# Root mean squares of the norms: summed on every partition by one matmul, and the power taken on 256 columns

## The chip, the cores and the metric

The kernel runs on one core of one Trainium2 chip. The metric is the device time of one execution in microseconds. In the traces PE is TensorE, PEld its weight loads, DVE is VectorE, ACT is ScalarE, POOL is GpSimd, SP is SyncE.

## What is computed

Two transformer blocks in fp32, one after the other, on 256 tokens of width 1024. The first has two layers with modulated norms, attention or retention, and a gated FFN, for the tokens x and, in its first layer, a context of 256 tokens (C in the kernel). The second has two layers of FFN, a mixing stage of three branches, and FFN. What the change touches is the norm:

```python
def rms_norm(x, g):
    xf = x.astype(jnp.float32)
    y = xf * lax.rsqrt(jnp.mean(xf * xf, axis=-1, keepdims=True) + EPS)
    return (y * g.astype(jnp.float32)).astype(x.dtype)

h_x = modulate(rms_norm(x, norm1_g[i]), mx[0], mx[1])     # first block
# retention, per head of width 512:
mu = jnp.mean(o, axis=-1, keepdims=True)
var = jnp.mean(jnp.square(o - mu), axis=-1, keepdims=True)
y = ((o - mu) * lax.rsqrt(var + EPS)) ...
# second block:
x = x + 0.5 * swiglu_2(rmsnorm(x, ffn1_norm[l]), ...)
h = rmsnorm(x, mix_norm[l])
```

## The kernel before

Activations stand with features on the partitions: a tensor of 256 tokens is 128 partitions x 8 feature tiles (`KC`) x 256 columns. So a norm needs, for each column (token), a sum over partitions and feature tiles, and its result on all partitions. The squares of the feature tiles are added up by VectorE into one tile of 128x256 (`acc`, L1782); what is left is the sum over partitions.

Weights stream through SyncE's DMA queue as raw 128x2048 fp32 tiles (3 buffers), and each block of 128x1024 is split into a high part by ScalarE (L346) and a low part by VectorE (L347), 4 buffers of each. A product is then three matmuls (L351 to L353: high times high, high times low, low times high) or, in the second block, two (L359, L360, the second on half the columns). Their results go to 4 PSUM banks (`pp`); small results go to 4 others (`pa`). A scheduler sets each engine's order of instructions by its own model of the times; an engine takes its instructions strictly in that order.

A norm takes these steps. `rstd_rs` (L381): two matmuls per part with `acc` as weights and two columns of ones put the sums of 128 tokens each on 128 partitions, as 128x2 (L389); VectorE scales and adds epsilon (L392); GpSimd raises to the power -0.5 (L394, `mhalf` holds -0.5). `rstd_ps` (L397): two matmuls with the result as broadcast weights and the identity bring it back onto the columns of all partitions (L401), in PSUM. `rstd_bc` (L405) copies that to SBUF on ScalarE (L407). fp32 matmuls of 128x2 and 128x128 leave two records each in the trace.

Who uses it: `norm_mod` (five norms of the first block; it reads the PSUM bank itself in `modulated`, L519: `mu` = x times gain, L528 `mt` = `mu` times the norm, L529 high part on ScalarE, L530 low part on VectorE); the four retention heads (`outputs`, first product L1396, queued among the matmuls that make the next head's keys, whose rotary products are L1307 and L1308); the four FFNs of the second block (`ffn`, L1178, on sums that were projected without the norm); the two mixing stages (L1521). All of them are generators: a `yield` marks where another stage's matmuls are put in between.

Of the kernel before, what the change touches and what calls it, by code (L numbers as in the profile page):

```python
# [8 lines left out]
F32 = mybir.dt.float32  # L9
# [3 lines left out]
ALU = mybir.AluOpType  # L13
# [3 lines left out]
D = 1024  # L17
KC = 8
T = 256
NF = 22  # L20
EPS = 1e-6
# [61 lines left out]
def _groups(n, gs):  # L83
    out, m = [], 0
    for g in gs:
        out.append(list(range(m, m + g)))
        m += g
    assert m == n, (m, n)
    return out
# [24 lines left out]
G_FFN = _groups(NF, FFN_GROUPS + [1] * (NF - sum(FFN_GROUPS)))  # L114
# [217 lines left out]
class _Kernel:  # L332
# [74 lines left out]
        self.nc.scalar.copy(bc, self.rstd_ps(rs))  # L407
        return bc

    def rstd_steps(self, acc, inv_n, out):  # L410

        rs = self.rstd_rs(acc, inv_n)
        yield
        out.append(self.rstd_bc(rs))
        yield

    def sumsq(self, src, pool):
# [7 lines left out]
    def run(self):  # L425
        tc, nc, A = self.tc, self.nc, self.A
        with ExitStack() as es:
            P = lambda name, bufs, **kw: es.enter_context(tc.tile_pool(name=name, bufs=bufs, **kw))
            self.p_pp = P("pp", 4, space=PSUM)
            self.p_pa = P("pa", 4, space=PSUM)  # L430
            self.p_dram = P("dram", 1, space=bass.MemoryType.DRAM)
            self.p_raw = P("raw", 3)
            self.p_hl = P("hl", 4)
            self.p_base = P("base", 1)
            self.p_sm = P("sm", 2)
            base = self.p_base

            self.vec = base.tile([128, VEC.n], F32, name="vec")
            self.load(self.vec, A["vec"])
            self.ident = base.tile([128, 128], F32, name="ident")  # L440
            self.ones = base.tile([128, 128], F32, name="ones")
            nc.vector.memset(self.ones, 1.0)
            self.mhalf = base.tile([128, 2], F32, name="mhalf")
            nc.vector.memset(self.mhalf, -0.5)
            self.eps = base.tile([128, 1], F32, name="eps")
            nc.vector.memset(self.eps, EPS)
            self.identb = base.tile([128, 128], BF16, name="identb")
            self.X = base.tile([128, KC, T], F32, name="X")
            self.hh = base.tile([128, KC, 512], F32R, name="hh")
            self.hl = base.tile([128, KC, 512], F32R, name="hl_")  # L450
            self.kvd = self.p_dram.tile([128, 4097], F32, name="kvd")

            with ExitStack() as e1:
                self.p_b1 = e1.enter_context(tc.tile_pool(name="b1", bufs=1))
                self.block1()
            if self.stop is None or self.stop.startswith("b2"):
                self.block2()
# [92 lines left out]
    def norm_mod(self, l, which, s, acc):  # L550


        rs = self.rstd_rs(acc, 1.0 / D)
        yield
        bc = self.rstd_ps(rs)
        G, sh = self.gain(l, s, 1 + 3 * which, f"{l}{s}{which}"), self.ada_p(l, s, 3 * which)
        src, o = (self.X, self.C)[s], slice(256 * s, 256 * s + 256)
        for k in range(KC):
            hi, lo = self.hps(k) if l == 1 and which == 1 else (self.hh[:, k, o], self.hl[:, k, o])
            self.modulated(k, hi, lo, src[:, k], bc, G[:, k:k + 1], sh[:, k:k + 1])  # L560
        yield
# [593 lines left out]
    def ffn(self, pool, ws, acc, scal, next_g):  # L1155


        nc = self.nc
        th = pool.tile([128, NF, 512], F32R, name="th", tag="th")
        norm, bc = None, []  # L1160
        if acc is not None:
            norm = self.rstd_steps(acc, 1.0 / D, bc)
        for grp in G_FFN:
            banks = [[self.pp() for _ in range(2)] for _ in grp]
            for k in range(KC):
                x = self.hp(k)
                for i in range(len(grp)):
                    for u in range(2):
                        self.mmp(banks[i][u], ws.next(), x, k == 0, k == KC - 1)
                if norm is not None and grp is G_FFN[0] and k in (2, 4):  # L1170
                    next(norm)
            for i, m in enumerate(grp):
                src = pool.tile([128, 512], F32, name="fn", tag="fn", bufs=2)
                for u in range(2):
                    self.halves(src[:, 256 * u:256 * u + 256], banks[i][u])
                if norm is not None:
                    v = src.rearrange("p (a q) -> p a q", a=2)
                    nc.vector.tensor_mul(v, v, bc[0].unsqueeze(1).to_broadcast([128, 2, 256]))  # L1178
                s = pool.tile([128, 256], F32, name="fs", tag="fs", bufs=2)
                nc.scalar.activation(s, src[:, 0:256], AF.Silu)  # L1180
                h = pool.tile([128, 256], F32, name="fh", tag="fh", bufs=2)
                nc.vector.tensor_mul(h, s, src[:, 256:512])
                self.split(th[:, m, 0:256], th[:, m, 256:512], h)
        out_g = self.v("final") if next_g is None and self.stop is None else None
        self.acc_x = _Acc(self, self.p_sm, "accx", KC, next_g is None)
        self.proj_p(ws, G_DOWN, NF, lambda k: th[:, k], self.resid_p(scal, next_g, out_g))
# [69 lines left out]
    def retention(self, pool, norm_c, mem, ec, ez):  # L1256
        nc, A = self.nc, self.A
# [8 lines left out]
        ws = self.stream("ret")  # L1266
        tmp = lambda w: pool.tile([128, w], F32, name="tmp", tag=f"tmp{w}", bufs=3 if w == 512 else 2)

        hd = [{} for _ in range(4)]

        def decay(h):
            Dm = hd[h]["D"] = pool.tile([128, 4, 256], F32, name="Dm", tag="Dm", bufs=1)
# [91 lines left out]
        def outputs(h):  # L1364

            Ph, Pl = hd[h]["P"]
            O = pool.tile([128, 4, 256], F32, name="O", tag="O")
            acc = tmp(256)
            for mp in range(2):
                ps = self.pa()  # L1370
                vh, vl = hd[h]["v"][mp]
                for j in range(2):
                    for kt in range(4):
                        ds = slice(128 * j, 128 * j + 128)
                        self.mm3(ps[:, 256 * j:256 * j + 256], (vh[:, kt, ds], vl[:, kt, ds]), (Ph[:, kt], Pl[:, kt]),
                                 kt == 0 and j == 0, kt == 3 and j == 1)
                nc.scalar.copy(O[:, 2 * mp:2 * mp + 2].rearrange("p a q -> p (a q)"), ps)
            nc.vector.tensor_add(acc, O[:, 0], O[:, 1])
            nc.vector.tensor_add(acc, acc, O[:, 2])
            nc.vector.tensor_add(acc, acc, O[:, 3])  # L1380
            yield
            mu = self.pa()
            nc.tensor.matmul(mu[:, 0:256], lhsT=self.ones, rhs=acc, start=True, stop=True)
            ac2 = _Acc(self, self.p_sm, "accg", 4)
            for m in range(4):
                nc.vector.scalar_tensor_tensor(out=O[:, m], in0=mu[:, 0:256], scalar=-1.0 / 512, in1=O[:, m],
                                               op0=ALU.mult, op1=ALU.add)
                ac2.add(O[:, m])
            yield
            rs = self.rstd_rs(ac2, 1.0 / 512)  # L1390
            yield
            bc = self.rstd_bc(rs)
            for m in range(4):
                i = 4 * h + m
                o = O[:, m]
                nc.vector.scalar_tensor_tensor(out=o, in0=o, scalar=self.v("gn", i), in1=bc, op0=ALU.mult, op1=ALU.mult)  # L1396
                nc.vector.tensor_mul(o, o, hd[h]["g"][:, m])
                self.split(zh[:, i], zl[:, i], o)
            yield
# [35 lines left out]
        norm = self.norm_mod(1, 1, 0, self.acc_x)  # L1435
# [38 lines left out]
    def mix(self, pool, l, acc):  # L1474
        nc, A = self.nc, self.A
        tmp = lambda w, nm, bufs=1: pool.tile([128, w], F32, name=nm, tag=nm, bufs=bufs)
        com, es = pool, ExitStack()
        pool = es.enter_context(self.pool(f"mixe{l}"))
# [24 lines left out]
        ws = self.stream(f"mix_{l}")  # L1503
# [8 lines left out]
        lru = (self.hl[:, :, 0:256], self.hl[:, :, 256:512])  # L1512

        bcs = []
        norm = self.rstd_steps(acc, 1.0 / D, bcs)

        def scaled(dsts):

            def ev(grp, ps, banks):
                for i, m in enumerate(grp):  # L1520
                    nc.vector.tensor_mul(dsts[m], ps[i], bcs[0])  # L1521
            return ev

        d = {4: kf, 9: vT}
# [114 lines left out]
                next(g)  # L1639
            running[:] = [g for g in running if next(g, self) is not self] + list(new)  # L1640

        self.proj(ws, [[0, 1]], KC, self.hps, 256, scaled(d), lambda gi, k: next(norm) if k in (3, 6) else None)
        advance(mem_job(0))
        self.proj(ws, [[2, 3]], KC, self.hps, 256, scaled(d))
        advance(mem_job(1))
# [96 lines left out]
        pool = es.enter_context(self.pool(f"mixl{l}"))  # L1742
# [43 lines left out]
class _Stream:  # L1786
# [33 lines left out]
    def next(self, n=1):  # L1820
        b, j = divmod(self.i, 8)
        assert j + n <= 8
        if b == self.b:
            self.split()
        self.i += n
        s = slice(128 * j, 128 * j + 128 * n)
        return self.hi[:, s], self.lo[:, s]
# [20 lines left out]
```

## Time and profile before

| | |
|---|---|
| time, median of 3 runs | 2456.08 us (2454.55 to 2456.79) |
| time of the profiled execution | 2456.09 us |
| its span | 2454.3 us |
| TensorE busy | 2419.2 us, 99% |
| VectorE busy | 1649.7 us, 67% |
| ScalarE busy | 1252.5 us, 51% |
| GpSimd busy | 70.2 us, 3%, 90 instructions |

The span is the traced part; the time holds 1.8 us more around it. The granted TensorE clock is at its upper level all through, so times of different stages can be compared directly. Matmuls overlap at their ends, so what one costs is read from the distance of starts, not from its own duration.

### The profile page before, as it was taken

What the parts mean: (1) busy time and instruction counts of PE and PEld (TensorE: products, weight loads), DVE (VectorE), ACT (ScalarE), POOL (GpSimd) and SP (SyncE); (2) the same over time, 40 slices, a digit from 0 to 9 for tenths busy, and PEclk for the clock granted to TensorE, in tenths of its full rate; (3) what the DMA queues carried; (4) which work ended last, traced back from release to release, by engine and by line L of the source; (5) the groups of instructions that cost most, each with busy time, mean ns of one, the idle gap of its engine ahead of it and who ended that gap; (6) DMA issues with size and microseconds to landing.
All of it is one profiled execution on the core that took longest, in us unless ns stands there. A gap on an engine that the chain in (4) does not pass through costs nothing.

```text
span 2454.3 us, 38056 instructions
## 1 busy us (share of the span) xinstructions
PE 2419.2 (99%) x15304; PEld 2108.0 (86%) x15304; DVE 1649.7 (67%) x2800; ACT 1252.5 (51%) x2173; POOL 70.2 (3%) x90
## 2 busy tenths in 40 slices
PE   7999999999999999999999999999999999999998
PEld 6666698777899999988888889998888888999887
DVE  7447477653366556676687678778768766877874
ACT  4546352222254444655555467455546546845653
POOL 2310000000000000000000100000000010000000
PEclk9999999999999999999999999999999999999999
DMA  8530445653232224555555534555555553355553
GB/s 303 217 121 1 148 146 199 230 220 105 102 113 86 104 104 154 194 188 186 181 188 189 201 109 156 184 189 185 192 178 185 190 209 110 129 198 189 182 193 106
DMA packets 57825, 402.72 MB, mean 164 GB/s; under 512 B 6464, under 2 KB 7616, under 8 KB 9904
## 3 DMA queue, kind: packets, MB, share of 16 engines
q1 hardware_dynamic: 55808, 393.54, 45.2%
q0 software_dynamic: 1408, 4.65, 0.6%
q8 instruction: 120, 1.97, 0.3%
q10 hardware_dynamic: 432, 2.10, 0.2%
q14 instruction: 57, 0.47, 0.1%
HBM read 397.12 MB, written 3.15 MB: 163 GB/s over the span
## 4 chain that ended last, share of the span: by engine, by line
PE 94%; DVE 3%; ACT 2%; issue 0%; DMA 0%; POOL 0%; SPq 0%; DVEq 0%; ACTq 0%
PE pp L359 26%; PE pp L360 13%; PE pp L351 13%; PE pp L353 13%; PE pp L352 13%; PE pp L1329 1%; PE pp L1331 1%; PE pp L1330 1%; PE pp L474 1%; PE pa L968 1%; PE pp L1003 1%; PE pa L967 1%; PE pp L1022 1%; ACT whi L346 1%; PE pa L352 0%; PE pa L351 0%
## 5 line engine op out<-in xcount | busy, mean ns | idle before, releaser
L347 DVE TENSOR_TENSOR wlo<-raw,whi 128x1024 fp32r<-128x1024 f32 (+1 forms) x645 | 787.7, 1223 | 392.0 <-ACT whi L346 384.3
L346 ACT CAST whi<-raw 128x1024 fp32r<-128x1024 f32 (+1 forms) x645 | 674.9, 1049 | 697.4 <-PE pp L352 336.5
L359 PE MATMUL pp<-hh,whi 128*128 128x512 f32 x1760 | 618.2, 394 | 0.0
L351 PE MATMUL pp<-hh,whi 128*128 128x256 f32 (+1 forms) x1608 | 515.3, 321 | 3.5 <-ACT whi L346 3.5
L353 PE MATMUL pp<-hh,wlo 128*128 128x256 f32 (+1 forms) x1608 | 513.1, 320 | 2.7 <-DVE wlo L347 2.7
L360 PE MATMUL pp<-hh,wlo 128*128 128x256 f32 x1760 | 490.8, 279 | 0.0
L359 PEld LDWEIGHTS pp<-hh,whi 128*128 128x128 f32 x1760 | 329.8, 187 | 79.4 <-DVE fn L1191 1.0
L351 PEld LDWEIGHTS pp<-hh,whi 128*128 128x128 f32 x1608 | 303.5, 189 | 42.5 <-issue 16.5
L360 PEld LDWEIGHTS pp<-hh,wlo 128*128 128x128 f32 x1760 | 329.9, 187 | 0.1
L353 PEld LDWEIGHTS pp<-hh,wlo 128*128 128x128 f32 x1608 | 303.4, 189 | 25.8 <-DVE wlo L347 3.5
L352 PE MATMUL pp<-hl__87,whi 128*128 128x512 f32 (+1 forms) x936 | 321.9, 344 | 0.0
L359 PE MATMUL pp<-th,whi 128*128 128x512 f32 x880 | 309.2, 393 | 0.0
L360 PE MATMUL pp<-th,wlo 128*128 128x256 f32 x880 | 248.9, 283 | 0.0
L352 PE MATMUL pp<-hh,whi 128*128 128x256 f32 x800 | 227.9, 285 | 0.0
L359 PEld LDWEIGHTS pp<-th,whi 128*128 128x128 f32 x880 | 165.3, 188 | 38.2
L352 PEld LDWEIGHTS pp<-hl__87,whi 128*128 128x128 f32 x936 | 176.1, 188 | 23.1 <-DVE hl__87 L530 0.2
L360 PEld LDWEIGHTS pp<-th,wlo 128*128 128x128 f32 x880 | 165.4, 188 | 0.0
L352 PEld LDWEIGHTS pp<-hh,whi 128*128 128x128 f32 x800 | 151.5, 189 | 0.7 <-issue 0.3
L1190 ACT COPY fn<-pp 128x256 f32<-128x256 f32 x220 | 82.0, 374 | 125.4 <-PE pp L360 125.4
L1191 DVE TENSOR_TENSOR fn<-pp,fn 128x256 f32<-128x256 f32 x220 | 92.0, 422 | 34.5 <-ACT fn L1190 34.5
L499 DVE SCALAR_TENSOR_TENSOR ada_acc<-raw,cact,ada_acc 128x1024 f32<-128x1024 f32 x56 | 70.4, 1281 | 28.0 <-DMA raw<-in_ada 27.4
L351 PE MATMUL pp<-th,whi 128*128 128x512 f32 (+1 forms) x198 | 73.5, 371 | 0.0
(394 smaller groups left out, 3540.9 us busy)
## 6 DMA issues: line engine op xcount, KB each, us to landing
raw<-in_b2ffn SPq DMA_DIRECT2D x132, 1024.0 KB, 4.9
raw<-in_mix SPq DMA_DIRECT2D x74, 1024.0 KB, 4.9
raw<-in_ffn SPq DMA_DIRECT2D x66, 1024.0 KB, 4.9
raw<-in_ada SPq DMA_DIRECT2D x40, 1024.0 KB, 4.9
raw<-in_ret SPq DMA_DIRECT2D x24, 1024.0 KB, 4.8
araw<-in_ada SPq DMA_DIRECT2D x8, 1024.0 KB, 8.5
raw<-in_reto SPq DMA_DIRECT2D x8, 1024.0 KB, 4.8
raw<-in_memkv SPq DMA_DIRECT2D x7, 1024.0 KB, 8.7
```

The source lines that it names most:

```text
L346: self.nc.scalar.copy(hi, src)
L347: self.nc.vector.tensor_tensor(out=lo, in0=src, in1=hi.bitcast(F32), op=ALU.subtract)
L351: nc.tensor.matmul(ps, lhsT=w[0], rhs=x[0], start=start, stop=False)
L352: nc.tensor.matmul(ps, lhsT=w[0], rhs=x[1], start=False, stop=False)
L353: nc.tensor.matmul(ps, lhsT=w[1], rhs=x[0], start=False, stop=stop)
L359: nc.tensor.matmul(bank, lhsT=w[0], rhs=xp, start=start, stop=False)
L360: nc.tensor.matmul(bank[:, 256:512], lhsT=w[1], rhs=xp[:, 0:256], start=False, stop=stop)
L474: nc.tensor.matmul(ps[32 * q:32 * q + 32, :], lhsT=self.cact[:, k, :], rhs=raw[:, 512 * q:512 * q + 512], start=k == 0, stop=k == KC - 1)
L499: nc.vector.scalar_tensor_tensor(out=acc[s][:, o], in0=raw[:, o], scalar=c, in1=acc[s][:, o], op0=ALU.mult, op1=ALU.add)
L967: nc.tensor.matmul(o, lhsT=qs[j][:, q], rhs=ks[:, kc, j, 512 - n:512], start=i == 0, stop=False)
L1190: self.nc.scalar.copy(out, bank[:, 256:512])
L1191: self.nc.vector.tensor_tensor(out=out, in0=bank[:, 0:256], in1=out, op=ALU.add)
```

## The change

15 of the 19 norms take another way; the memory's norm, the two at the start and the last one keep the old one. A function `rstd(acc, inv)` does one fp32 matmul with a constant matrix as weights (128x128, every element 1/1024, or 1/512 in the retention) and the sums of squares, 128x256, as moving operand: each partition of the PSUM bank then holds the mean of every column. VectorE adds epsilon on the way to SBUF, 128x256; GpSimd raises this tile to the power -0.5 in place. The matmuls with the identity and ScalarE's copy are left out. In `norm_mod` the product now reads SBUF. In the FFN and the mix all of it is queued in one step, at k = 2 or k = 3, where there were two.

```diff
-    def rstd_steps(self, acc, inv_n, out):
-        rs = self.rstd_rs(acc, inv_n)
-        yield
-        out.append(self.rstd_bc(rs))
+    def rstd(self, acc, inv):
+        nc = self.nc
+        ps = self.pa()
+        n = len(acc.parts)
+        for i, p in enumerate(acc.parts):
+            nc.tensor.matmul(ps[:, 0:256], lhsT=inv, rhs=p, start=i == 0, stop=i == n - 1)
+        bc = self.p_sm.tile([128, 256], F32, name="bc", tag="bc")
+        nc.vector.tensor_scalar(out=bc, in0=ps[:, 0:256], scalar1=EPS, scalar2=None, op0=ALU.add)
+        nc.gpsimd.tensor_tensor(out=bc, in0=bc, in1=self.mhalf[:, 0:1].to_broadcast([128, 256]), op=ALU.pow)
+        return bc
+
+    def rstd_steps(self, acc, out):
+        out.append(self.rstd(acc, self.inv))
         yield
...
+            self.inv = base.tile([128, 128], F32, name="inv")
+            nc.vector.memset(self.inv, 1.0 / D)
...
     def norm_mod(self, l, which, s, acc):
-        rs = self.rstd_rs(acc, 1.0 / D)
+        bc = self.rstd(acc, self.inv)
         yield
-        bc = self.rstd_ps(rs)
...
-                if norm is not None and grp is G_FFN[0] and k in (2, 4):
+                if norm is not None and grp is G_FFN[0] and k == 2:
                     next(norm)
...
             yield
-            rs = self.rstd_rs(ac2, 1.0 / 512)
+            bc = self.rstd(ac2, inv512)
             yield
-            bc = self.rstd_bc(rs)
             for m in range(4):
...
-        self.proj(ws, [[0, 1]], KC, self.hps, 256, scaled(d), lambda gi, k: next(norm) if k in (3, 6) else None)
+        self.proj(ws, [[0, 1]], KC, self.hps, 256, scaled(d), lambda gi, k: next(norm) if k == 3 else None)
```

On DVE, at the C norm of FFN 0 (`fh`, L1125, is a gated product of the FFN itself, `tl` its low part), before:

```order
L392 TENSOR_SCALAR ms<-pa 128x2 [waits PE_49]
L528 TENSOR_TENSOR mt<-mu,pa 128x256 [waits PE_49,Activation_49]
L528 TENSOR_TENSOR mt<-mu,pa 128x256 [waits Activation_49]
L524 TENSOR_SCALAR mu<-C,G_3104 128x256 [waits DVE_49]
L530 SCALAR_TENSOR_TENSOR hl__87<-mt,ada_103,hh 128x256 [waits Activation_49]
L528 TENSOR_TENSOR mt<-mu,pa 128x256 [waits DVE_49]
L1125 TENSOR_TENSOR fh<-fs,pp 128x256 [waits Activation_49]
```

and with the change, where L418 is the addition of epsilon, L540 and L542 are the old L528 and L530:

```order
L418 TENSOR_SCALAR bc<-pa 128x256 [waits PE_49]
L540 TENSOR_TENSOR mt<-mu,bc 128x256 [waits Activation_49,Pool_49]
L540 TENSOR_TENSOR mt<-mu,bc 128x256 [waits Activation_49]
L536 TENSOR_SCALAR mu<-C,G_3096 128x256 [waits DVE_49]
L542 SCALAR_TENSOR_TENSOR hl__89<-mt,ada_105,hh 128x256 [waits Activation_49]
L540 TENSOR_TENSOR mt<-mu,bc 128x256 [waits DVE_49]
```

The first product waits for Pool instead of PE; `fh` has moved further down.

On DVE, at the norm of the first retention head (L1307 and L1308 are the rotary products of the next head's keys, read from the PSUM banks, L1396 and L1397 the norm's and the gate's products, `zl` the low part of their result), before, from the row behind the addition of epsilon:

```order
L392 TENSOR_SCALAR ms<-pa 128x2 [waits PE_49,Pool_49]
L1307 TENSOR_TENSOR tmp<-pp,ctR 128x256 [waits PE_49]
L1308 TENSOR_TENSOR tmp<-pp,ctR 128x256
L1307 TENSOR_TENSOR tmp<-pp,ctR 128x256 [waits PE_49]
L1308 TENSOR_TENSOR tmp<-pp,ctR 128x256
L1311 TENSOR_TENSOR tmp<-tmp 128x256 [waits DVE_49]
L1396 SCALAR_TENSOR_TENSOR O<-O,vec,bc 128x256 [waits Activation_49]
```

and with the change, where L1408, L1409 and L1320 are the old L1396, L1397 and L1307:

```order
L418 TENSOR_SCALAR bc<-pa 128x256 [waits PE_49]
L1408 SCALAR_TENSOR_TENSOR O<-O,vec,bc 128x256 [waits Pool_49]
L1408 SCALAR_TENSOR_TENSOR O<-O,vec,bc 128x256
L1409 TENSOR_TENSOR O<-O,sg 128x256 [waits DVE_49] x2
L1408 SCALAR_TENSOR_TENSOR O<-O,vec,bc 128x256
L347 TENSOR_TENSOR zl<-O,zh 128x256 [waits Activation_49]
L1409 TENSOR_TENSOR O<-O,sg 128x256 [waits DVE_49]
L1408 SCALAR_TENSOR_TENSOR O<-O,vec,bc 128x256
L1320 TENSOR_TENSOR tmp<-pp,ctR 128x256 [waits PE_49]
```

The norm's products, the first of which waits for Pool, now stand ahead of all rotary products.

## Rows read from the trace of the kernel before

**Rows 1.** The page: the chain that ended last, shares by engine.
```profile
PE 94%; DVE 3%; ACT 2%; issue 0%; DMA 0%; POOL 0%; SPq 0%; DVEq 0%; ACTq 0%
```

**Rows 2.** Groups by shape on POOL: count | busy us, mean ns | idle before, releaser.
```profile
L866 POOL TENSOR_TENSOR xn<-qg,ctA 128x256 f32<-128x256 f32 x8 | 5.9, 733 | 44.7 <-ACT qg L928 44.7
L683 POOL CAST identb<-ident 128x128 bf16<-128x128 f32 x1 | 0.3, 283 | 5.2 <-DMA ident<-in_k_common 5.2
L1839 POOL MEMSET const-float32-1.0<- 128x1 f32 x1 | 0.1, 101 | 0.0
```

**Rows 3.** One line, the pow: count, minimum/median/maximum in ns, first and last start.
```profile
L394 POOL TENSOR_TENSOR rs<-ms,mhalf x19: 688/697/1637, 26.0 to 2445.7; 128x2 f32<-128x2 f32 x19
```

**Rows 4.** Timeline of PE at the first changed norm: start us, us, instruction.
```profile
319.10 0.28 PE L353 MATMUL pp<-hh,wlo 128*128 128x256 f32 x1
...
319.58 0.36 PE L351 MATMUL pp<-hh,whi 128*128 128x256 f32 x1
...
321.70 0.28 PE L353 MATMUL pp<-hh,wlo 128*128 128x256 f32 x1
...
322.18 0.37 PE L351 MATMUL pp<-hh,whi 128*128 128x256 f32 x1
```

**Rows 5.** Timeline of PE around the mean of a retention head.
```profile
773.64 0.40 PE L352 MATMUL pp<-hl__87,whi 128*128 128x512 f32 x1
...
774.58 0.40 PE L353 MATMUL pp<-hh,wlo 128*128 128x512 f32 x1
774.82 0.59 PE L1383 MATMUL pa<-tmp,ones 128*128 128x256 f32 x2
...
775.48 0.40 PE L352 MATMUL pp<-hl__87,whi 128*128 128x512 f32 x1
```

**Rows 6.** Timeline of PE at the C norm of FFN 0; idle before it in brackets.
```profile
336.32 0.71 PE L401 MATMUL pa<-ident,rs 128*128 128x128 f32 x4 [0.44 <-POOL rs L394]
```

**Rows 7.** Timeline of POOL: pows in their order.
```profile
319.99 0.70 POOL L394 TENSOR_TENSOR rs<-ms,mhalf 128x2 f32<-128x2 f32 x1 [167.46 <-DVE ms L392]
...
697.74 0.69 POOL L394 TENSOR_TENSOR rs<-ms,mhalf 128x2 f32<-128x2 f32 x1 [361.48 <-DVE ms L392]
...
711.93 0.71 POOL L394 TENSOR_TENSOR rs<-ms,mhalf 128x2 f32<-128x2 f32 x1 [6.99 <-DVE ms L392]
780.87 0.69 POOL L394 TENSOR_TENSOR rs<-ms,mhalf 128x2 f32<-128x2 f32 x1 [68.22 <-DVE ms L392]
...
959.24 1.64 POOL L394 TENSOR_TENSOR rs<-ms,mhalf 128x2 f32<-128x2 f32 x1 [55.17 <-DVE ms L392]
1002.02 0.69 POOL L394 TENSOR_TENSOR rs<-ms,mhalf 128x2 f32<-128x2 f32 x1 [41.14 <-DVE ms L392]
...
1199.73 0.71 POOL L394 TENSOR_TENSOR rs<-ms,mhalf 128x2 f32<-128x2 f32 x1 [188.98 <-DVE ms L392]
```

**Rows 8.** Timeline of DVE beside two of these pows.
```profile
320.02 1.25 DVE L347 TENSOR_TENSOR wlo<-raw,whi 128x1024 fp32r<-128x1024 f32 x1
...
959.10 1.22 DVE L347 TENSOR_TENSOR wlo<-raw,whi 128x1024 fp32r<-128x1024 f32 x1
```

**Rows 9.** Timeline of DVE: first low parts of X and C for FFN 0.
```profile
324.98 1.27 DVE L530 SCALAR_TENSOR_TENSOR hl__87<-mt,ada,hh 128x256 fp32r<-128x256 f32 x3
...
338.14 0.48 DVE L530 SCALAR_TENSOR_TENSOR hl__87<-mt,ada,hh 128x256 fp32r<-128x256 f32 x1
```

**Rows 10.** Timeline of PE where a normed input is first read.
```profile
703.55 0.28 PE L351 MATMUL pp<-hh,whi 128*128 128x256 f32 x1
...
722.25 0.39 PE L351 MATMUL pp<-hh,whi 128*128 128x512 f32 x1
...
1008.93 0.49 PE L359 MATMUL pp<-hh,whi 128*128 128x512 f32 x1
```

**Rows 11.** Timeline of DVE behind the first head's norm: last read of a keys bank.
```profile
788.39 0.43 DVE L347 TENSOR_TENSOR kl<-pp,kh 128x256 fp32r<-128x256 f32 x1
```

**Rows 12.** Timeline of DVE: first product with the norm in an FFN.
```profile
1207.02 0.68 DVE L1178 TENSOR_TENSOR fn<-fn,bc 128x512 f32<-128x512 f32 x1
```

More of the change, by code (lines that the diff above doesn't have):

```diff
@@ L1161, in ffn @@
         if acc is not None:
-            norm = self.rstd_steps(acc, 1.0 / D, bc)
+            norm = self.rstd_steps(acc, bc)
         for grp in G_FFN:
@@ L1269, in retention @@
         hd = [{} for _ in range(4)]
+        inv512 = pool.tile([128, 128], F32, name="inv512")
+        nc.vector.memset(inv512, 1.0 / 512)
         def decay(h):
@@ L1514, in mix @@
         bcs = []
-        norm = self.rstd_steps(acc, 1.0 / D, bcs)
+        norm = self.rstd_steps(acc, bcs)
         def scaled(dsts):
```

## Prediction, made before the run

> **What bounds the kernel now.** I read the page first: TensorE is busy 99% of the span, VectorE 67%, GpSimd 3% (table above), and TensorE carries 94% of the chain that ended last [rows 1]. So a TensorE instruction that goes is worth its whole length, and work on another engine is free as long as no matmul has to wait for it. Next I read how long each operation of a norm takes on its engine [rows 2 to 5], then where TensorE waited for a norm. Of the 15 norms that change, one shows it: the C norm of the first FFN, where the broadcast matmuls waited 0.44 us for the pow [rows 6]. Last I read, norm by norm, when the result is first wanted [rows 9 to 12]. The reader should see there that the pow is short today and that most norms have only a few microseconds between it and the matmul that needs it.
>
> **What goes.** Each norm drops the group that sums the squares: the pass before it ends its matmul at 319.10 and goes on at 319.58, where 0.12 us is its normal step, so the group costs 0.36 us. The broadcast group, 321.70 to 322.18, costs 0.36 us too [rows 4]. In their place stands one fp32 matmul of 256 columns with the constant as weights. The trace has that shape once per head, the mean of a retention head: from 774.58 to 775.48 two matmuls of 512 columns and it take 0.90 us; just before, four such steps take 0.94 us (773.64 to 774.58), two 0.47, so it costs 0.43 us [rows 5]. TensorE saves 0.72 - 0.43 = 0.29 us per norm, 15 x 0.29 = 4.4 us. All of it is on the path, since TensorE has no idle time there to swallow it. On VectorE the addition of epsilon grows from 128x2 (0.16 us) to 128x256, and is put at twice the time, so the pow starts 0.2 us later; ten small copies leave ScalarE. Neither engine is a bound.
>
> **What comes: a pow on 128x256, price P, 15 times.** The trace has the pow only on 128x2, where it takes 0.69 us undisturbed (688 to 697 ns for the lower half of 19) [rows 3]. The price on 128 times as many columns is the one number that decides, and it is bounded far apart.
> From below: the columns behind the first two cost no more than in a GpSimd multiplication, which takes 0.73 us for 256 columns [rows 2]. With (0.73 - 0.19)/256 = 2.1 ns per column that is 0.69 + 254 x 0.0021 = 1.2 us. The 0.19 us of fixed time is an estimate between the 0.10 us of a MEMSET with one column and the 0.28 us of a CAST with 128 [rows 2].
> From above: the 0.69 - 0.19 = 0.50 us that the pow takes beyond the fixed time is all work on its two columns, one after the other. Then P = 0.19 + 128 x 0.50 = 64 us.
> That a two-column pow takes as long as a 256-column multiplication says that its arithmetic is long; how much of it overlaps from column to column no row tells. With ends a factor of 53 apart, and no row nearer to one than to the other, I take the middle on a ratio scale, the root of 1.2 x 64: P = 9 us.
> The Trainium skill (GPSIMD Engine Reference, section 3.1) gives about 2.6 cycles per element for GpSimd's two-input elementwise instructions, and at the clock it states that is an estimate of 0.55 us for 256 columns, as the multiplication's row has it. By that rule alone the pow would be at the lower end, and the sum would be that of the first rival below; the rule doesn't say that it holds for pow.
>
> **What each norm can hide.** After the pow a norm's chain is short, so I compare the moment of first need with the start of the pow (its start before plus 0.2 us). In a norm with modulation it is a product, a ScalarE pass and a subtraction of 128x256, each under 0.5 us [rows 9], together 1.4 us. VectorE takes its queue in order: the first product now waits for GpSimd and holds the splits of weights behind it, but these run some 3 blocks ahead, so the norm's own need comes first.
> - X norm of FFN 0, pow at 320.2 [rows 7]: behind the broadcast group three steps of 9 matmuls of 0.12 us are left of the pass before, so TensorE turns to X at 322.18 + 3.24 = 325.4 [rows 4], just when the first low part is done (three of them take 1.27 us from 324.98 [rows 9]). Less 1.4 us, P is hidden up to 3.8; the split queued in front leaves 3.5.
> - C norm of FFN 0: the matmul that waited for the pow starts at 336.32 [rows 6], so the pow began at 335.55, and will at 335.75. The pass over X has 96 matmuls of 0.12 us from 325.5 on, with the norm's groups and gaps some 13.1 us, so C is wanted at 338.6, and its low part was done at 338.6 [rows 9]. Hidden: 1.5.
> - X norm of the retention, pow at 697.95, wanted at 703.55: 4.2. Its C norm, 712.1, wanted at 722.25: 8 (8.7 less what is queued). X norm of the second FFN, 1002.25, wanted at 1008.9: 5 [rows 7, 10].
> - Retention heads 0 to 2. Here the order changes to the worse: the rotary products of the next keys used to stand ahead of the first use of the norm, and now stand behind it. They and the key splits (the last read of a bank starts at 788.39 [rows 11]) free the two PSUM banks that the second half of the values takes; its first half is 96 matmuls of 0.12 us, 11.5 us, and starts when the keys end near 782.3, so it takes them at 793.9. From the pow's end to that last read the new queue holds about 20 instructions of 0.38 us, 7.6 us; so the pow must end by 786.3, having begun at 781.0 [rows 7]: 5.4 hidden, each.
> - Head 3, pow at 959.4: it is wanted as features 12 to 15 of the output projection, whose step takes 4 x 3 x 0.12 = 1.44 us; the sums go out at k = 5, so k = 12 comes six steps, 8.6 us, behind the pow's start. Less product, gate product and split, 2.5 us: 6.
> - The four FFN norms: first product at 1207.02, 7.1 us behind a pow at 1199.9 [rows 7, 12]; behind it in the queue stands the read of the fourth bank, which TensorE wants one group (16 pairs of 0.24 + 0.12 us, 5.8 us) later; less the queue between, about 9. The two mix norms have their first use later still, and I put them at 15, which the sum doesn't use.
> Beyond that, TensorE waits microsecond for microsecond.
>
> **The sum** at P = 9: 5.5 + 7.5 + 4.8 + 1 + 4 = 22.8 us for the five modulated norms, 3 x 3.6 + 3 = 13.8 us for the heads, nothing for FFN and mix: 36.6 us. The profiled execution takes 2456.09 us (span 2454.3 plus 1.8 around it), within 0.01 us of the median 2456.08. 2456.1 - 4.4 + 36.6 = **2488 us**, 1.3% slower. The change breaks even at P = 4.5 (1 + 3 + 0.3 = 4.3 us lost), and is 0.2% slower from P = 5.7 on. About 0.2% is what a measurement of this kernel can tell from no change.
>
> **Rivals.**
> *Everything hidden.* If P lies at or below 3, near the multiplication's price, at most 1.5 us is lost at the C norm and the 4.4 us stay: 2452 to 2453 us, with the 0.44 us wait gone at best 2451. For it: the GpSimd row of that shape. Against it: 0.69 us for two columns. Up to P = 5.7 the result stays under +0.2%. This is the end on the other side, not slower.
> *Serial.* At P = 64 each site's cover is a trifle: 15 x 64 - 110 us of cover = 850 us, so 3301 us; at P = 30 the loss is 340 us and the time 2791.
> *GpSimd held by VectorE.* A pow took 1.64 us where a split of weights had begun 0.14 us before it; with the split begun 0.03 us after it, the pow took its 0.70 us [rows 7, 8]. If a long pow is held by every split that comes in its time (1.22 us of the 2.88 us that a block of 24 matmuls lasts), 9 us become 9/(1 - 0.42) = 15.6 and the loss 124 us: 2575 us.
> The Trainium skill (GPSIMD Engine Reference, section 8) says that GpSimd shares its SBUF interfaces with VectorE, in contention with VectorE instructions of two SBUF inputs. The rows agree for one of the two meetings, and don't tell who yields when GpSimd's instruction is the long one.
>
> **How the numbers follow.** Hidden up to P = 5.7: 0.38. The middle, P from 5.7 to 30 (2461 to 2791 us), the port's case among it: 0.42, with 2488 for its middle. Serial, above 30: 0.20. The predicted time is 2488. The range leaves out only the serial case: from 2450 (all hidden and the wait gone, with the spread of the runs) to 2791. Slower by over 0.2%: 0.42 + 0.20 = 0.62. Faster by over 0.2% needs 4.9 us, more than the sum holds with everything hidden (4.4 + 0.44), so only with luck in the order: 0.08. Within 0.2%: 0.30.
>
> **What would show it.** The row of the new pow gives P at once; between 5 and 12 us the middle holds. TensorE's idle time should name GpSimd or the products behind it at the two norms near 320 and 336 first, then at 698 and 1002, then the banks near 794, and not at the mix. The new matmul should cost TensorE 0.43 us. Wrong would be: a P near 1 us, and then the gain; losses at FFN norms with a P below 9, which would mean that the splits' lead is smaller than I read; or TensorE waiting for VectorE while GpSimd is done, which would be the port.

## The result, and the profile after

The changed kernel takes 3005.9 us (3005.44 to 3007.4), against 2456.3 us: a ratio of 1.224 with a 95% interval of 1.2219 to 1.2261. It is 550 us slower. The direction was forecast, the size not: 2488 us were predicted, and 3006 lies above the range that ended at 2791.

The page of the changed kernel, busy time by engine and the chain, to be read against [rows 1] and the table above:

```profile
PE 2442.2 (81%) x15214; PEld 2124.6 (71%) x15214; DVE 1650.9 (55%) x2802; ACT 1248.0 (42%) x2163; POOL 678.4 (23%) x90
...
PEclk9999779999778977779998989997997997999799
...
PE 72%; POOL 18%; DVE 4%; issue 3%; ACT 3%; DMA 0%; SPq 0%; DVEq 0%; POOLq 0%; ACTq 0%
PE pp L359 20%; POOL bc L419 18%; PE pp L360 10%; PE pp L351 10%; PE pp L352 10%; PE pp L353 10%; DVE wlo L347 1%; ACT whi L346 1%; PE pp L486 1%; PE pa L979 1%; PE pp L1342 1%; PE pp L1014 1%; PE pp L1343 1%; PE pa L978 1%; PE pp L1344 1%
```

TensorE does nearly the same work and is busy 81% instead of 99%; GpSimd goes from 70 to 678 us, and its one line, the new pow L419, carries 18% of the chain. The line of the granted clock, all nines before, falls to 7 or 8 in the slices in which TensorE stands still longest. The pow itself, from the view of that line (count, minimum/median/maximum in ns), which answers [rows 3]:

```profile
L419 POOL TENSOR_TENSOR bc<-bc,mhalf x15: 41116/41122/42050, 319.3 to 2779.6; 128x256 f32<-128x256 f32 x15
```

P is 41.1 us, 60 times the pow on 128x2. Where it went, from the timeline of PE (start, duration, instruction, in brackets the idle time before it and what ended it); there is one such row per norm, and three heads, four FFNs and two mixes look alike:

```profile
362.43 0.58 PE L351 MATMUL pp<-hh,whi 128*128 128x256 f32 x1 [38.27 <-ACT hh L541]
...
416.69 0.58 PE L351 MATMUL pp<-hh,whi 128*128 128x256 f32 x1 [39.61 <-ACT hh L541]
...
820.45 0.58 PE L351 MATMUL pp<-hh,whi 128*128 128x256 f32 x1 [37.93 <-ACT hh L541]
...
874.09 0.58 PE L353 MATMUL pp<-hh,wlo 128*128 128x256 f32 x1 [37.97 <-DVE wlo L347]
...
987.41 0.55 PE L1342 MATMUL pp<-whi,hh 128*128 128x256 f32 x1 [33.87 <-DVE kl L347]
...
1269.37 0.58 PE L351 MATMUL pp<-zh,whi 128*128 128x256 f32 x1 [35.92 <-ACT zh L346]
...
1349.90 0.79 PE L359 MATMUL pp<-hh,whi 128*128 128x512 f32 x1 [37.00 <-DVE hh L542]
...
1354.63 0.79 PE L359 MATMUL pp<-hh,whi 128*128 128x512 f32 x1 [2.45 <-ACT memv L823]
...
1590.74 0.77 PE L359 MATMUL pp<-hh,whi 128*128 128x512 f32 x1 [31.65 <-ACT th L346]
...
1809.41 1.19 PE L1575 MATMUL pa<-mk,cq 128*128 128x256 f32 x2 [34.21 <-issue]
```

None of these rows names GpSimd. The releaser is the last link, a high part on ScalarE, a low part on VectorE, a split of weights; at the mix the profile names none (`issue`). What all of them had waited for stands in the view of L419, under who waited for it (line, us in total, times): at each of the 15 norms the first product on VectorE that reads the result, `cq` being that of the mix.

```profile
  DVE mt L540: 204.6, 5
  DVE O L1408: 164.9, 4
  DVE fn L1189: 138.1, 4
  DVE cq L1533: 70.3, 2
```

At the first head the chain of waits between 940 and 990 us shows it (start, length, piece):

```profile
939.86 0.43 DVE bc L418
940.43 41.13 POOL bc L419
981.58 0.88 DVE O L1408 x2
...
987.41 0.55 PE pp L1342
```

The waits at the 15 norms, the small ones right behind them included, sum to 526 us. TensorE's busy time grows by 23.0 us although it has fewer matmuls. 2456 + 526 + 23 = 3005 us: the whole difference.

### The profile page after: what moved, and what is told of

Its sections match the earlier page's. It is cut to its first block, busy times and chain, and to the rows that moved or that the text cites. A ratio compares the mean times of both kernels' runs of the same rounds, so it can differ in the third digit from the quotient of the medians.

```text
span 3003.7 us, 37864 instructions
## 1 busy us (share of the span) xinstructions
PE 2442.2 (81%) x15214; PEld 2124.6 (71%) x15214; DVE 1650.9 (55%) x2802; ACT 1248.0 (42%) x2163; POOL 678.4 (23%) x90
## 4 chain that ended last, share of the span: by engine, by line
PE 72%; POOL 18%; DVE 4%; issue 3%; ACT 3%; DMA 0%; SPq 0%; DVEq 0%; POOLq 0%; ACTq 0%
PE pp L359 20%; POOL bc L419 18%; PE pp L360 10%; PE pp L351 10%; PE pp L352 10%; PE pp L353 10%; DVE wlo L347 1%; ACT whi L346 1%; PE pp L486 1%; PE pa L979 1%; PE pp L1342 1%; PE pp L1014 1%; PE pp L1343 1%; PE pa L978 1%; PE pp L1344 1%
## 5 line engine op out<-in xcount | busy, mean ns | idle before, releaser
L419 POOL TENSOR_TENSOR bc<-bc,mhalf 128x256 f32<-128x256 f32 x15 | 620.4, 41360 | 1679.8 <-DVE bc L418 1679.7
L359 PE MATMUL pp<-hh,whi 128*128 128x512 f32 x1760 | 629.1, 399 | 165.8 <-ACT th L346 126.3
L359 PEld LDWEIGHTS pp<-hh,whi 128*128 128x128 f32 x1760 | 335.1, 190 | 248.9 <-ACT th L346 127.5
L351 PEld LDWEIGHTS pp<-hh,whi 128*128 128x128 f32 x1608 | 307.1, 191 | 160.1 <-ACT hh L541 116.4
L353 PEld LDWEIGHTS pp<-hh,wlo 128*128 128x128 f32 x1608 | 306.9, 191 | 64.3 <-DVE wlo L347 41.7
L360 PEld LDWEIGHTS pp<-hh,wlo 128*128 128x128 f32 x1760 | 335.2, 190 | 0.2
L1342 PE MATMUL pp<-whi,hh 128*128 128x256 f32 x256 | 75.1, 293 | 101.7 <-DVE kl L347 101.7
L352 PEld LDWEIGHTS pp<-hh,whi 128*128 128x128 f32 x800 | 151.4, 189 | 0.8 <-issue 0.3
L1189 DVE TENSOR_TENSOR fn<-fn,bc 128x512 f32<-128x512 f32 x88 | 61.0, 693 | 141.0 <-POOL bc L419 138.1
```

The source lines that it names most:

```text
L351: nc.tensor.matmul(ps, lhsT=w[0], rhs=x[0], start=start, stop=False)
L352: nc.tensor.matmul(ps, lhsT=w[0], rhs=x[1], start=False, stop=False)
L353: nc.tensor.matmul(ps, lhsT=w[1], rhs=x[0], start=False, stop=stop)
L359: nc.tensor.matmul(bank, lhsT=w[0], rhs=xp, start=start, stop=False)
L360: nc.tensor.matmul(bank[:, 256:512], lhsT=w[1], rhs=xp[:, 0:256], start=False, stop=stop)
L419: nc.gpsimd.tensor_tensor(out=bc, in0=bc, in1=self.mhalf[:, 0:1].to_broadcast([128, 256]), op=ALU.pow)
```

## The experiments

**The pow taken out.** The same kernel with a cheap operation of the same shape in its place.

```diff
-        nc.gpsimd.tensor_tensor(out=bc, in0=bc, in1=self.mhalf[:, 0:1].to_broadcast([128, 256]), op=ALU.pow)
+        nc.gpsimd.tensor_tensor(out=bc, in0=bc, in1=self.eps[:, 0:1].to_broadcast([128, 256]), op=ALU.mult)
```

> The change, with the pow on 128x256 replaced by a multiplication of the same shape on GpSimd (by a constant of 1e-6; the power is left out, so the norm's values are not the reference's). Theory A, the pow's price is all of the loss: the multiplication takes about 0.73 us, below every cover (the smallest is 1.5 us), so the wait is gone everywhere and TensorE keeps its 15 x 0.29 = 4.4 us: 2451 to 2453 us. Theory B, part of the loss comes from the new order of VectorE's instructions or from the longer addition of epsilon, whatever the pow takes: TensorE still waits at several of the 15 norms, 2458 us or more.

Measured: 2446.2 us, a ratio of 0.9955 (0.9942 to 0.9967), so 10 us faster than before, and 5 us below the range of theory A. The operation takes 0.61 us (median, in the view of its line):

```profile
L419 POOL TENSOR_TENSOR bc<-bc,eps x15: 602/612/1526, 319.1 to 2251.3; 128x256 f32<-128x256 f32 x15
```

No wait above 0.25 us is left at a norm beyond those for the sums of squares that the kernel before has too. Theory B falls: the new order and the longer addition cost nothing that shows. The gain is larger than 4.4 us, and the timeline of PE at the first FFN norm shows why:

```profile
1191.68 0.28 PE L360 MATMUL pp<-hh,wlo 128*128 128x256 f32 x1
1191.79 0.59 PE L416 MATMUL pa<-accx,inv 128*128 128x256 f32 x2
1192.04 0.58 PE L359 MATMUL pp<-hh,whi 128*128 128x512 f32 x1
1192.46 0.28 PE L360 MATMUL pp<-hh,wlo 128*128 128x256 f32 x1
```

From 1191.68 to 1192.46, 0.78 us, stand a step of 0.12, a step of 0.24 and the new matmul: 0.42 us, where 0.43 was predicted. But I had read the old groups only up to the start of the matmul behind them, and that one is also held 0.08 us. In the kernel before, at the first norm, the matmul behind the two of [rows 4] is this one:

```profile
319.78 0.28 PE L352 MATMUL pp<-hl__87,whi 128*128 128x256 f32 x1
```

From 319.10 to 319.78 stand two steps of 0.12 us and the group: 0.44 us, not 0.36. So a norm saves 2 x 0.44 - 0.42 = 0.46 us, 15 norms 6.9 us. By the distances between the norms' groups in the two traces, four stretches between neighbouring norms give 0.42 to 0.50 us each, the three that lead from one head to the next 0.71 to 0.73 us, and the two that lead from a mix to the FFN behind it 0.90 us; what goes beyond 0.46 there stays unexplained. The 0.44 us wait goes too, and, behind the second mix, some 1.6 us more that the profiled execution of the kernel before lost at the lower clock level behind a wait at 2008 us (last section): its clock was not at the upper level all through.

**The long pow alone, in the kernel before.**

```diff
+        if wide:
+            nc.gpsimd.tensor_tensor(out=self.wide, in0=ms[:, 0:1].to_broadcast([128, 254]),
+                                    in1=self.mhalf[:, 0:1].to_broadcast([128, 254]), op=ALU.pow)
         nc.gpsimd.tensor_tensor(out=rs, in0=ms, in1=self.mhalf, op=ALU.pow)
```

> The kernel before (its matmuls, its order of work, its 128x2 pow), with one more pow, on 128x254, put ahead of the real one on GpSimd at the same 15 norms; nothing reads its result. Theory A, the length of the pow alone makes the loss, wherever the rest stands: about 41 us at each of the 15 norms, with covers like those of the change, so within 25 us of the changed kernel, 2985 to 3030 us. Theory B, the new queue order carries a good part: clearly less, 2900 us or below.

Measured: 3074.1 us, ratio 1.2517 (1.2498 to 1.2536). Theory B falls. Theory A's cause holds, its number is missed by 44 us on the upper side: the same pow costs more in the old form than in the changed kernel. The timeline of PE at the first head:

```profile
950.84 0.39 PE L353 MATMUL pp<-hh,wlo 128*128 128x512 f32 x1
990.74 1.22 PE L404 MATMUL pa<-ident,rs 128*128 128x128 f32 x4 [39.51 <-POOL rs L397]
```

Here the broadcast matmul L404 (L401 before) stands in TensorE's own queue, so TensorE soon stops, and 39.5 of the 41.5 us that the two pows take (40.81 and 0.69) show. In the changed kernel no instruction of TensorE waits for GpSimd itself; TensorE goes on until it needs a later result, and 33.9 us show. So the changed form, without the second matmul group, hides 5.6 us more at a head. The waits at the norms sum to 583 us here; all idle time of TensorE grows by 582 us and its busy time by 34.8: 2456 + 582 + 35 = 3073 us, against 3072.5 in the profiled execution.

**Narrower pows.** The power on 32 or on 16 columns, a multiplication on the rest.

```diff
-        nc.gpsimd.tensor_tensor(out=bc, in0=bc, in1=self.mhalf[:, 0:1].to_broadcast([128, 256]), op=ALU.pow)
+        nc.gpsimd.tensor_tensor(out=bc[:, 0:32], in0=bc[:, 0:32], in1=self.mhalf[:, 0:1].to_broadcast([128, 32]), op=ALU.pow)
+        nc.gpsimd.tensor_tensor(out=bc[:, 32:256], in0=bc[:, 32:256], in1=self.eps[:, 0:1].to_broadcast([128, 224]), op=ALU.mult)
```

> The change, with the pow on 32 of the 256 columns and a multiplication by 1e-6 on the other 224 (their power is left out). Theory A, the pow costs 0.37 us and 0.159 us per column, in line from 2 to 256 columns: the pow row reads 5.5 us, pow and multiplication 6.1 us, and with the covers read from the changed kernel (3.8, 1.5, 4.0, 3.2, 4.1 at the modulated norms, 7.3 and 5.3 at the heads, 9.5 and 7.4 at FFN and mix) the loss is 2.3 + 4.6 + 2.1 + 2.9 + 2.0 + 0.8 = 14.7 us: 2466 us, up to 2470 with TensorE's clock after the waits. Theory C, the pow works in blocks of columns or has a large start-up that the wide one repays: a row well off 5.5 us (above 8 or below 3).

> The change, with the pow on 16 of the 256 columns and a multiplication by 1e-6 on the other 240 (their power is left out). Theory A as revised by the first runs: the pow costs 0.32 us and 0.159 us per column, so its row reads 2.9 us, with the multiplication 3.5 us; at the two modulated norms where a split of weights stands ahead it is held to 4.4 us. Against covers of 3.8, 1.5, 4.0, 3.2 and 4.1 us that leaves waits of 0.6, 2.0, 0.4, 0.3 and 0 us, 3.3 us, with up to 2 us of half clock behind the longest. From the 2446.2 us of the run without a pow: 2450 to 2454 us, below the kernel before. Theory E, any pow on many columns costs more than its own length (it holds VectorE's splits): 2458 us or more.

Measured: 2478.6 us with 32 columns, 1.009 (1.0077 to 1.0104), and 2459.8 us with 16, 1.0018 (1.0009 to 1.0026); 8.6 us over the upper end of the one, 5.8 us over that of the other. The pow's row came as expected. With 32 columns, from the timeline of POOL at the X norm of FFN 0, where a split of weights holds it, and at the C norm:

```profile
321.90 6.34 POOL L419 TENSOR_TENSOR bc<-bc,mhalf 128x32 f32<-128x32 f32 x1 [167.81 <-DVE bc L418]
...
341.89 5.42 POOL L419 TENSOR_TENSOR bc<-bc,mhalf 128x32 f32<-128x32 f32 x1 [13.13 <-DVE bc L418]
```

and with 16, at the second FFN's X norm:

```profile
1006.94 2.90 POOL L419 TENSOR_TENSOR bc<-bc,mhalf 128x16 f32<-128x16 f32 x1 [38.01 <-DVE bc L418]
```

0.69 us for 2 columns, 2.90 for 16, 5.42 for 32, 40.81 for 254 and 41.12 for 256 lie on one line: 0.159 us per column and 0.33 to 0.42 us besides. Theory C falls; a column costs the same among 2 as among 256. With 16 columns the time lies where theory E put it (2458 us or more), but not for E's reason: the splits of weights that begin during a pow are not held. This one begins in the pow at the first FFN norm and takes its usual time:

```profile
1210.31 1.23 DVE L347 TENSOR_TENSOR wlo<-raw,whi 128x1024 fp32r<-128x1024 f32 x1 [1.68 <-ACT whi L346]
```

Against the run without a pow, TensorE's idle time grows by 9.8 us with 16 columns, where waits of 3.3 us were expected, and its busy time by 5.3 us. What the expectations missed are above all two prices behind the wait. The first is the clock. These are the stretches of PE in the run with 16 columns, behind waits of 3.1 and 1.9 us (length, busy, granted clock, DMA):

```profile
1017.00:1021.00 4.00, 3.89 (x14) 0.61 0.93 352
341.30:346.00 4.70, 4.56 (x23) 0.64 0.63 218
324.00:330.00 6.00, 4.90 (x37) 1.00 0.07 29
```

The granted clock has two levels, 1.00 (2.4 GHz) and 0.50 (1.2 GHz), and the figure is the mean of the stretch. Behind the wait of 3.1 us it is 0.61, behind that of 1.9 us 0.64, so most of each stretch ran at the lower level; the third stretch, with waits of 0.6 and 0.4 us in it, keeps 1.00. TensorE's busy time grows over that of the run without a pow by 5 us with 16 columns (two waits of 1.9 us or more at the norms), by 15 us with 32 (six of 1.8 us or more) and by 35 us in the changed kernel (15 of over 30 us): an estimate of 2 to 3 us for each such wait. The second is a wait of another piece of work. From the timelines of PE and of ACT around the X norm of the second FFN, with 16 columns:

```profile
1017.11 0.51 PE L359 MATMUL pp<-hh,whi 128*128 128x512 f32 x1 [3.09 <-ACT memv L824]
```

```profile
1010.88 0.91 ACT L542 ACTIVATE hh<-mt,ada 128x256 fp32r<-128x256 f32 x2 [2.66 <-DVE mt L541]
...
1016.24 0.82 ACT L824 ACTIVATE memv<-pp,rs 128x256 f32<-128x256 f32 x2
```

The copies `memv` of the memory branch empty a PSUM bank that the FFN wants next. They stand on ScalarE behind the high parts, and those wait for the norm. So this norm hides 0.4 us (3.5 on GpSimd, 3.1 waited), not 4.1. At the nine norms of heads 0 to 2, FFN and mix, where the cover is 7 us or more, neither run shows a wait for the norm.

**The power on other engines.** Square root on ScalarE and reciprocal on VectorE; or exp(-0.5 ln) on ScalarE.

```diff
-        nc.vector.tensor_scalar(out=bc, in0=ps[:, 0:256], scalar1=EPS, scalar2=None, op0=ALU.add)
-        nc.gpsimd.tensor_tensor(out=bc, in0=bc, in1=self.mhalf[:, 0:1].to_broadcast([128, 256]), op=ALU.pow)
+        nc.scalar.activation(bc, ps[:, 0:256], AF.Sqrt, bias=self.eps)
+        nc.vector.reciprocal(bc, bc)
...
+        nc.scalar.activation(bc, ps[:, 0:256], AF.Ln, bias=self.eps)
+        nc.scalar.activation(bc, bc, AF.Exp, scale=-0.5)
```

> The change with the power taken off GpSimd: ScalarE takes the square root of the mean plus epsilon straight from PSUM, VectorE the reciprocal, both on 128x256. If only the engine of the power was wrong, the chain is a table load of 1.28 us, a pass of 0.4 us and a reciprocal of 0.4 to 1.7 us, about 2 to 3.5 us, of which the C norm of FFN 0 shows 0.5 to 2 us; TensorE keeps 4.4 us: 2452 to 2456 us. Against it: two table loads per norm on ScalarE, in front of the high parts of the weights, could hold the splits and bring 2460 us or more.

> The change with the power as exp(-0.5 ln(mean + epsilon)), both on ScalarE, straight from PSUM; GpSimd and VectorE have no part. Two passes of 0.4 to 0.5 us and one or two table loads of 1.28 us, 2.2 to 3.5 us, against 1.28 + 0.4 + 1.75 = 3.4 us of square root and reciprocal. If the chain's length at the modulated norms is what counts, between 2447 (one table for both) and 2451 us (two tables); if ScalarE's own time counts (its table loads in front of the splits' high parts), above 2452 us.

Measured: 2450.0 us for the square root, 0.9975 (0.9965 to 0.9985), and 2452.4 us for ln and exp, 0.9988 (0.9979 to 0.9997). The first is faster than both kernels, by 0.25% against the kernel before, and 2 us below its expected range. The second lies between the 2451 us of two tables and the 2452 us from which ScalarE's own time was to count, and its interval (2450.4 to 2454.8 us) holds both, so the time doesn't decide between them. Its groups on ACT (count | busy, mean ns) show two table loads at every norm:

```profile
L418 ACT ACT_TABLE_LOAD x15 | 19.2, 1283 | 0.3
L419 ACT ACT_TABLE_LOAD x15 | 19.2, 1283 | 0.3
```

In both, the modulated norms of FFN 0 and of the retention still make TensorE wait, 0.3 to 1.7 us at a time, and with ln and exp the copies of the memory branch 1.9 us. The longest, at the C norm of FFN 0, with the square root and then with ln and exp, from the timelines of PE:

```profile
338.65 0.50 PE L351 MATMUL pp<-hh,whi 128*128 128x256 f32 x2 [1.37 <-ACT hh L541]
...
340.68 0.38 PE L351 MATMUL pp<-hh,whi 128*128 128x256 f32 x1 [1.65 <-ACT hh L541]
```

**So those four norms were left as they were**, the other 11 taken by square root:

```diff
     def norm_mod(self, l, which, s, acc):
-        bc = self.rstd(acc, self.inv)
+        old = not (l == 1 and which == 1)
+        bc = self.rstd_rs(acc, 1.0 / D) if old else self.rstd(acc, self.inv)
         yield
+        if old:
+            bc = self.rstd_ps(bc)
```

> Square root on ScalarE and reciprocal on VectorE at 11 norms (retention heads, FFNs, mixes and the modulated X norm of the second FFN), the kernel before's norm at the other four modulated ones. In the kernel with square roots everywhere those four and what lies between cost TensorE 2.4 us more than before, by the starts of its norm groups (-1.02 us at 319, +1.40 us at 780), though their matmuls save 1.8; so the old form there should bring 2.4 us: 2447 to 2449 us. If the loss between 319 and 780 belongs to something else (the run's DMA, the order), it stays at 2450 us.

Measured: 2447.6 us, 0.9968 (0.9955 to 0.998), 8 us under the kernel before and the fastest version found that takes the power. By time the gain over square roots everywhere is not clear of noise: 0.9968 and 0.9975 lie within each other's intervals. The trace shows it: by the starts of the norms' groups the stretch from 319 to 780 us, which square roots made 2.4 us longer, is as long as in the kernel before to 0.1 us. Of the 15 norms only the C norm of FFN 0, in its old form, shows a wait for the power (from the timeline of PE), the one of [rows 6]:

```profile
335.84 0.71 PE L401 MATMUL pa<-ident,rs 128*128 128x128 f32 x4 [0.45 <-POOL rs L394]
```

## Why the prediction was wrong in size and right in kind

- **The step that failed is the price of the pow.** It was bounded by 1.2 and 64 us, rightly: 41.1 us lies between. But then I took 9 us, the middle on a ratio scale, and gave the serial rival 0.20, which put it outside the range; neither number had a row behind it. One width can't separate a start-up from a price per column, and the trace had only one. The serial rival (P above 30) is what happened. Its own size, 64 us, was off by the fixed part: of the 0.69 us of two columns 0.37 are fixed and 2 x 0.16 the columns', where I took 0.19 fixed and 2 x 0.25. Why a column costs 0.159 us no run shows. The direction, slower, came out right because the break-even of 4.5 us lay far below the real price; the 9 us had no part in it.
- **The time that follows from the right P.** With my covers and P = 41.1 the loss is 15 x 41.1 - 110 = 507 us, and the time 2456 - 4 + 507 = 2959 us. The measured 3006 differs by 47 us: 19 us of waits (526 us, not 507), 35 of the clock, less 8 that the profiled execution without a pow saved above the estimate (12 us, not 4.4); the rest is rounding. So the mechanism, P less the cover at each norm, held.
- **The covers** held within 1 us for five of nine kinds. Predicted and read (P less the wait): X and C of FFN 0, 3.5 and 3.8, 1.5 and 1.5; X of the retention 4.2 and 4.0; head 3, 6 and 5.3; FFN 9 and 9.5. Heads 0 to 2 hid more than predicted, 7.3 and not 5.4. Three were far too large: the C norm of the retention (8 and 3.2), where a split held behind the product ended the wait (`wlo`, at 874.09), not the norm's own need; the mix (15 and 7.4, which at P = 9 the sum did not use); and the X norm of the second FFN, 5 predicted, 4.1 read at the first wait, but 1.7 with the second one behind it. "these run some 3 blocks ahead, so the norm's own need comes first" was true of FFN 0 and not of the retention's C norm.
- **The clock** was left out. Behind each of the 15 waits TensorE works for some microseconds at the lower level: 35 us in all, by its busy time against the run without a pow. Behind the wait at the first FFN norm of the changed kernel (length, busy, granted clock, DMA):

```profile
1590.70:1594.70 4.00, 3.96 (x12) 0.50 0.72 262
```

- **The saving** of 4.4 us was too small, since the matmul behind each old group was held as well: about 6.9 us by the groups alone.
- **The port** plays no part beyond the start. The pow took 42.05 us where a split had begun 0.17 us before it, 41.96 us at two norms where it had begun 0.23 us before, 41.6 us at the two mixes where it had begun 0.62 us before, and 41.1 us at the other ten. At the first FFN norm it began at 1546.92, and on the timeline of DVE in the changed kernel the splits that begin during it take their usual time, while the pow takes 41.14 us:

```profile
1548.44 1.23 DVE L347 TENSOR_TENSOR wlo<-raw,whi 128x1024 fp32r<-128x1024 f32 x1 [1.68 <-ACT whi L346]
1551.23 1.23 DVE L347 TENSOR_TENSOR wlo<-raw,whi 128x1024 fp32r<-128x1024 f32 x1 [1.56 <-ACT whi L346]
```

  So a split already running makes the pow longer by up to 0.9 us, about what is left of the split. A pow that is running neither holds a split nor is held by one: all twelve splits that begin during a pow, at the FFN and mix norms, take 1.22 to 1.23 us. The rival in which a long pow is held by every split falls. The Trainium skill (GPSIMD Engine Reference, section 8) names the contention with VectorE instructions of two SBUF inputs; these rows agree only for the start.
- **The rule for two-input instructions** (the Trainium skill, GPSIMD Engine Reference, section 3.1: about 2.6 cycles per element) does not reach to pow here. At the 1.2 GHz of its section 1, 0.159 us per column is an estimate of 190 cycles. The measurement decides.

## What to carry to other kernels

Before an operation on GpSimd is made wider, put its time over two widths on a line, with one spare instruction in a trace if need be; a row of one shape alone can't tell a start-up from a price per column, and on 128 times the columns the two differ by 40 us. Spreading values over partitions by a matmul before an expensive elementwise step, and back by another, can be worth two matmul groups: here 0.46 us per norm against 41. And a cover is not only the distance to the result's own reader: everything that stands behind the waiting instruction on its engine, and on the engine behind that, has its own reader on the bottleneck.

## What was not expected of the hardware

- GpSimd's pow takes 0.159 us per column of 128 partitions and 0.33 to 0.42 us besides (0.69 us for 2 columns, 41.12 us for 256). That is 75 times the 2.1 ns that the prediction estimated for a multiplication's column.
- TensorE's mean granted clock over the next 4 to 5 us was 0.61 behind a wait of 3.1 us and 0.64 behind one of 1.9 us, and it stayed at 1.00 behind 0.6 us; by the estimate above each such fall cost 2 to 3 us beside the wait. A wait of 1.45 us was seen with both outcomes, and no run shows what decides between them. In the kernel before, the stretches of PE behind two such waits (length, busy, granted clock, DMA):

```profile
1384.90:1388.90 4.00, 4.00 (x34) 1.00 0.78 221
2008.60:2012.60 4.00, 4.00 (x22) 0.59 0.84 218
```

- A reciprocal on VectorE takes 1.75 us on 128x256, four times a product of that shape (0.42 us). With the square root, the group on DVE (count | busy, mean ns | idle before):

```profile
L419 DVE RECIPROCAL bc<-bc 128x256 f32<-128x256 f32 x15 | 26.2, 1750 | 5.2 <-ACT bc L418 5.2
```
